# A hybrid decoder block on one NeuronCore: operands opened inside a convolution, a row root in two pieces, V's turns and the last square in another place

## The chip, the cores and the metric

The kernel runs on one core of a Trainium2 chip. A core has engines with instruction queues of their own: TensorE (PE: matmuls, and PEld, the loading of their stationary operand), VectorE (DVE), ScalarE (ACT), GpSimd (POOL) and SyncE (SP, which here only issues DMAs). They run side by side and wait for each other through semaphores. Matmuls add into PSUM banks; everything else lies in SBUF, and DMA queues move data between it and the chip's memory.

The metric is the time of the kernel on the device in microseconds (us), the median over its runs.

## The reference

One layer of a decoder block on x of 1 x 1024 x 1024 in float32, cut to what matters here:

```python
h = rms_norm(x, mix_norm_g)
z_a, q, k, v, gate_logits = split(h @ w_in)          # 1024 x 5888
u, vv = split(gelu(z_a))                             # 768 channels each
vv = rms_norm(vv)                                    # over the 768 channels
y_a = u * (causal 128x128 mixing of vv, per chunk and channel group, + b_s)
q, k = partial_rope(q, positions), partial_rope(k, positions)
y_b = dilated_mixture_attention(q, k, v)             # groups (128,1), (512,4), (2048,16)
merged = sigmoid(g_a) * (y_a @ w_branch_a) + sigmoid(g_b) * (y_b @ w_branch_b)
x = x + merged @ w_out
up = rms_norm(x) @ w_up                              # 1024 x 5632
a, val = up[:, :2816], up[:, 2816:]
a = causal_depthwise_conv(a, conv_w, conv_b)         # three taps along the sequence
x = x + (gelu(a) * val) @ w_down                     # 2816 x 1024
return rms_norm(x, final_norm_g)
```

## The kernel before, in words

**Products.** A float32 product is made of three matmul passes. Each operand is split into an upper part, which ACT makes by a copy to a reduced type (`to_parts`, L168; in the input projection `in_split`, L307), and a lower part, the difference from the upper one, which DVE or POOL makes (L169, L308). The passes are upper by upper, lower weight by upper, and upper weight by lower (`HIGH_FIRST`), so a product of four blocks of 128 rows has twelve matmuls with 512 columns, and its first four need only the upper parts. The three big projections besides do seven products instead of eight for a 2 x 2 partition of their operands, named P1 to P7. The operands of P6, P7 and P5 are sums or differences of the quarters (of the weights: `weight_sums`, L270 to L280; of the left operand: S1 to S4), and the results are put together by adds on DVE that read a PSUM bank. Three products go on in the bank of another one: P2 in that of P1, P4 in that of P7, P3 in that of P5.

**Order.** The order of PE is written out by hand over the whole kernel. Work between matmuls is placed with `after(lag, ...)`, which runs it when `lag` ticks have gone by; a tick is six matmuls of a product. On DVE and ACT the order is written out by hand at the start (up to the tenth product in `in_order`), from the merge to the end of the fourth unit of the up projection, and over the end of the up projection, the beginning of the down projection and its last product. In the later stretches lower parts on DVE stand in a list, `waiting`, and `low(n)` lets `n` of them go. Elsewhere a scheduler places DVE and ACT; POOL is left to it throughout. Queues run in the order they are given: SP issues most DMAs, ACT and POOL a few.

**Stages.** (1) `beginning()`: the first two units of the input projection run as plain products on x while its row norms are made; a unit is a pair of 128-column blocks of `w_in`. For each half of the sequence, `square_row` sums squares on ACT, `root` (L384) turns four columns of sums (one for each block of 128 rows) into the row scale on POOL, in two instructions (L387, L388), `diagonal` puts the scale on a diagonal (on DVE, L397, for the first half; on ACT, L399, for the second), `spread` (L405) broadcasts it with matmuls, and `scale_x` scales the transposed x. `in_left` then splits the quarters and sums of x, and S1 to S4. (2) `in_product` (L512, its matmuls L523, its adds L543 to L552) does the other units product by product; `in_ahead` loads and opens their weights, and `meanwhile(i)` (L1201) holds what is done on DVE and ACT beside the first sixteen products. `chain` in it is a list of small steps on DVE and ACT that make the rotary tables out of the positions; `some(n)` does the next n of them, `wide` and `turns` finish the tables. Units 0 to 2 are V of the spatial gating (kind "zv"): `turn_v` (L635) turns it with four PE transposes (L640) and ACT's Gelu out of PSUM (L645), `norm_v` and `spatial` go on from there. Rope (`turned`, L725) follows each "qa" unit. (3) Attention, the spatial gating and the gates run beside the units; then the merge and the output projection. (4) The up projection: `up_product` (L1864, matmuls L1875) with a unit of gate and value columns at a time. Its order has, for unit ff, P6(ff), P1(ff+1), P7(ff), P5(ff), P2(ff+1), P4(ff), P3(ff), without P1 and P2 of unit ff + 1 in the first units. `up_ahead` loads weights and opens operands: the sums on POOL (L275, L276, L277; on DVE in units 1 and 4), the upper part on ACT (L168), the lower part on DVE for P2, P5 and P4 and otherwise on POOL (on DVE in units 1 and 4 and for P1 of the first three). After P2 and P4 `convolve` (L1800) does the causal convolution: a first tap on ACT (L1809), two taps on DVE (L1813, L1817), and the Gelu on ACT (L1806); P4 and P3 then multiply on POOL (L1908 and L1912). `sums_g` (L1834) makes sums of finished columns for the down projection. (5) The down projection (`down_step`, L2134); with its last product, P3, each block of 128 rows ends in `down_done`: an add (L2202), `square` (L2159), `finish_block` with `finish_rms` (L2255, the root on POOL), a scaling on ACT (L2167) with ACT's DMA issue (L2168), one on DVE and SP's DMA issue.

`up_product` has a parameter `beside`, a function that `convolve` calls ahead of its Gelu. The first units use it in places (`beginning_up`), and so do P4 of the units behind the last P2; the loop from L2090 on does not use it up to the last P2.

## Time and profile before

| what | value |
| --- | --- |
| median of 3 runs | 1381.47 us (1381.35 to 1382.63) |
| profiled execution | 1382.45 us |
| its span, from the first instruction to the last | 1380.7 us |
| PE, 0 to 26 us / 26 to 140 us, busy | 24.34 of 26 / 111.47 of 114 us |
| PE, 140 to 770 us, busy | 629.3 of 630 us |
| PE, 770 to 1160 us, busy | 386.77 of 390 us |
| PE, 1160 to 1373 us, busy | 212.82 of 213 us |
| ACT, share of the span that it is busy | 47% |
| POOL, share of the span that it is busy | 22% |

The profile is that of one execution. "Busy" is time in which an engine computes; issuing a DMA, waiting and branching are not counted. A line of the profile names the line of the kernel, the engine, the operation, output and inputs by their names in the program (buffer numbers left out), and shapes. What stands in brackets behind a row is the idle time of that engine just before and the event that ended it. The granted clock is the share of full speed at which PE was let run; a matmul with 512 columns starts 0.227 us after the one before it at clock 1.00, and 0.43 us at 0.51. In a row of a timeline, an instruction's time is that from its start to its end, and instructions of one line that follow each other are shown as one piece with their count. Pieces of PE overlap a little, as matmuls are pipelined, so lengths of products are read from start to start.

### The profile page before, as it was taken

The numbers are of one execution on the slowest core, as the hardware profiler recorded it, in microseconds if no ns is written. First come the engines' busy times: TensorE is split into PE (matmuls) and PEld (weight loads), VectorE is DVE, ScalarE is ACT, GpSimd is POOL, SyncE is SP. The second block draws the span as 40 slices with busy tenths as digits, with TensorE's granted clock in tenths as the row PEclk, the third lists the DMA queues.
The fourth block names the chain that finished last, engine by engine and source line by source line (L and its number), as shares of the span: only waits on it lengthen the run. The fifth ranks groups of instructions, "written<-read, shape, count | busy, mean of one in ns | idle before, by whom it ended". The sixth has DMA issues, their size and how long they took to land.

```text
span 1380.7 us, 19226 instructions
## 1 busy us (share of the span) xinstructions
PE 1364.7 (99%) x6428; PEld 1129.2 (82%) x6428; DVE 1033.8 (75%) x1884; ACT 655.8 (47%) x1294; POOL 300.8 (22%) x295
## 2 busy tenths in 40 slices
PE   9999999999999999999999999999999999999997
PEld 7777888888888888888888886888888888888886
DVE  7978687777877887759789877666766667676674
ACT  8782455555543334444456344333333335454453
POOL 0111000000230000220011235665556643000002
PEclk9999999999999999999999999999999999999999
DMA  9435443554537995884741133233333327986663
GB/s 353 92 95 165 135 137 117 141 174 124 142 102 270 319 298 192 281 291 145 251 147 60 61 99 115 92 115 115 105 102 106 123 97 252 391 312 221 198 206 122
DMA packets 144595, 237.01 MB, mean 172 GB/s; under 512 B 13808, under 2 KB 58608, under 8 KB 144496
## 3 DMA queue, kind: packets, MB, share of 16 engines
q1 hardware_dynamic: 141968, 231.53, 50.5%
q0 software_dynamic: 1088, 2.10, 0.9%
q10 hardware_dynamic: 1440, 2.16, 0.4%
q8 instruction: 51, 0.84, 0.3%
q14 instruction: 48, 0.39, 0.1%
HBM read 167.77 MB, written 64.29 MB: 168 GB/s over the span
## 4 chain that ended last, share of the span: by engine, by line
PE 80%; DVE 8%; DMA 5%; issue 3%; ACT 2%; POOL 1%; SPq 1%; POOLq 0%; DVEq 0%; ACTq 0%
PE in_P L523 23%; PE uP L1875 17%; PE dn L2134 13%; PE up L1875 7%; PE pa L1348 5%; PE wo_P L1709 4%; PE pu L868 2%; PE pu L1855 2%; PE pb L1348 2%; DMA wd<-in_w_down_dram 1%; DMA YC<-in_x_dram 1%; PE pp L852 1%; DMA wT<-wd 1%; DMA X<-in_xt_dram 1%; DVE wd L1019 1%
## 5 line engine op out<-in xcount | busy, mean ns | idle before, releaser
L523 PE MATMUL in_P<-R,G 128*128 128x512 f32 x1008 | 246.1, 395 | 0.4 <-ACT C L543 0.3
L523 PEld LDWEIGHTS in_P<-R,G 128*128 128x128 f32 x1008 | 184.8, 188 | 37.3 <-ACT C L543 0.8
L2134 PE MATMUL dn<-R 128*128 128x512 f32 x924 | 209.6, 389 | 0.0
L2134 PEld LDWEIGHTS dn<-R 128*128 128x128 f32 x924 | 173.5, 188 | 36.0
L168 ACT ACTIVATE R<-up 128x512 fp32r<-128x512 f32 x130 | 78.5, 626 | 128.2 <-DVE up L277 42.1
L307 ACT ACTIVATE G<-wr 128x512 fp32r<-128x512 f32 x126 | 79.0, 628 | 102.2 <-PE in_P L523 63.4
L1875 PE MATMUL uP<-R 128*128 128x512 f32 x504 | 122.0, 391 | 2.7 <-POOL R L169 2.1
L523 PE MATMUL in_P<-G,G 128*128 128x512 f32 x504 | 122.2, 393 | 0.2 <-DVE C L550 0.2
L1875 PE MATMUL up<-G,R 128*128 128x512 f32 x504 | 121.5, 391 | 0.5 <-ACT R L168 0.3
L1875 PE MATMUL uP<-G,R 128*128 128x512 f32 x504 | 121.6, 390 | 0.0
L1875 PEld LDWEIGHTS uP<-R 128*128 128x128 f32 x504 | 94.7, 188 | 23.1 <-POOL R L169 2.5
L1875 PEld LDWEIGHTS up<-G,R 128*128 128x128 f32 x504 | 94.5, 188 | 21.8 <-ACT R L168 0.8
L308 DVE TENSOR_TENSOR G<-wr,G 128x512 fp32r<-128x512 f32 x126 | 88.4, 703 | 30.8 <-ACT G L307 29.8
L1875 PEld LDWEIGHTS uP<-G,R 128*128 128x128 f32 x504 | 94.5, 188 | 20.5 <-ACT R L168 0.4
L523 PEld LDWEIGHTS in_P<-G,G 128*128 128x128 f32 x504 | 92.9, 188 | 19.8 <-issue 1.2
L169 POOL TENSOR_TENSOR R<-up,R 128x512 fp32r<-128x512 f32 x55 | 84.6, 1538 | 71.8 <-ACT R L168 71.8
L169 DVE TENSOR_TENSOR R<-up,R 128x512 fp32r<-128x512 f32 x75 | 64.0, 855 | 20.7 <-ACT R L168 20.5
L168 ACT ACTIVATE R<-db 128x512 fp32r<-128x512 f32 x77 | 48.0, 625 | 56.4 <-PE dn L2134 46.8
L169 DVE TENSOR_TENSOR R<-db,R 128x512 fp32r<-128x512 f32 x77 | 53.7, 701 | 25.9 <-ACT R L168 25.7
L1348 PE MATMUL pa<-R,G 128*128 128x512 f32 x288 | 67.9, 389 | 0.0
L1348 PEld LDWEIGHTS pa<-R,G 128*128 128x128 f32 x288 | 54.1, 188 | 11.2
L523 PE MATMUL in_P<-G 128*128 128x512 f32 x252 | 62.6, 394 | 0.4 <-DVE C L552 0.2
(282 smaller groups left out, 2402.5 us busy)
## 6 DMA issues: line engine op xcount, KB each, us to landing
wr<-in_w_in_dram SPq DMA_DIRECT2D x44, 512.0 KB, 4.3
up<-in_w_up_dram SPq DMA_DIRECT2D x44, 512.0 KB, 3.6
dA<-gd SPq DMA_DIRECT2D x55, 256.0 KB, 4.8
wd<-in_w_down_dram SPq DMA_DIRECT2D x44, 256.0 KB, 5.5
wT<-wd SPq DMA_DIRECT2D x44, 256.0 KB, 3.9
dS<-gS SPq DMA_DIRECT2D x44, 256.0 KB, 4.3
db<-wT SPq DMA_DIRECT2D x44, 256.0 KB, 4.7
gd<-Y SPq DMA_DIRECT2D x42, 256.0 KB, 2.0
```

Of the source, the lines that this page charges most:

```text
L168: nc.scalar.activation(hi, src, AF.Copy)
L169: fn = lambda: lo_eng.tensor_tensor(lo, src, f32(hi), ALU.subtract)
L307: lambda: nc.scalar.activation(op[:, 0], src, AF.Copy),
L308: lambda: nc.vector.tensor_tensor(op[:, 1], src, f32(op[:, 0]), ALU.subtract),
L523: nc.tensor.matmul(acc, op[:, w, kt, :], left[LEFT[name], kt][:, a, :], start=opened and i == 0, stop=i == len(HIGH_FIRST) - 1, skip_group ...
L852: nc.tensor.transpose(pp[:, i * P : (i + 1) * P], self.pr[:, h, s * P : (s + 1) * P], ident)
L868: nc.tensor.matmul(pu[:, h * HD : (h + 1) * HD], self.pT[:, i, :], vt[:, h * HD : (h + 1) * HD], start=i % n == 0, stop=i % n == n - 1,)
L1348: nc.tensor.matmul(acc, unit[a][kt // 4][:, kt % 4, :], two(R, 8 * h + kt)[:, b, :], start=n == 0 and i == 0, stop=n == len(kts) - 1 and i ...
L1709: nc.tensor.matmul(acc, left[LEFT[name], kt][:, a, blk * P : (blk + 1) * P], out_ops[s][:, w, :], start=name not in SHARED and kt == 0 and ...
L1855: nc.tensor.matmul(acc, plain_up[which, k][:, w, kt, :], left[f"A{h + 1}{k + 1}", kt][:, a, :], start=n == 0 and i == 0, stop=n == KT - 1 ...
L1875: nc.tensor.matmul(acc, op[:, w, kt, :], left[LEFT[name], kt][:, a, :], start=opened and i == 0, stop=i == len(HIGH_FIRST) - 1, skip_group ...
L2134: nc.tensor.matmul(accs[blk], dops[s][:, 0, a, blk * P : (blk + 1) * P], dops[s][:, 1, w, :], start=SEQ[j] not in CONTINUES and kt == 0 an ...
```

## The change

The changes, by the place at which they take effect:

- `root` works on the first three columns and then on the fourth, with four POOL instructions instead of two, for each half of x.
- In `beginning`, three matmuls more (`plain_step`) go ahead of `spread(0)`; steps of the rotary chain stand at other places; the DMA that loads the positions is a step of that chain, behind the one that loads `chan`. For the first unit with seven products (unit 2) the sums for P6 stand where its split stood, ahead of P1, and P6's split behind the sum for P4. `in_op` leaves out sums that are made already (`summed`).
- In `meanwhile`, unit 2's P7 is split around S3's parts; the last lower part of S1 and of A22 stands one product later, behind that product's add; unit 3's P6 has its sums at i = 6 and its split one tick later; the ends of the rotary chain, `wide` and `turns` stand one product later.
- V's turns: those of unit 2 come 4 to 6 ticks after the result instead of 2 or 3, those of unit 0 one tick later. Rope comes 12 ticks after its loads instead of 10.
- In the up projection, P2 of unit 5 and P4 of unit 4 open an operand inside `convolve`, ahead of the Gelu.
- `finish_rms` takes the engine of its second small step: DVE in the last norm, POOL as before in the one ahead of the up projection.
- In `down_done`, the last square of a block stands ahead of the scaling and storing of the block before it.

```diff
@@ -291,7 +291,10 @@
         weight_sums(st_a, st_v, t3s, key, name, t3_tile, sum_eng)
         to_parts(op[:, 0], op[:, 1], weight_src(st_a, st_v, t3s, key, name), lo_eng)
 
+    summed = set()
+
     def in_sums(n, name):
+        summed.add((n, name))
         weight_sums(
             raws[n, 0], raws.get((n, 1)), in_t3, n, name,
             lambda: wt.tile([P, HALF], F32, name=f"wt3_{n}", tag="t3", bufs=1), nc.vector,
@@ -309,7 +312,8 @@
         )
 
     def in_op(n, name):
-        in_sums(n, name)
+        if (n, name) not in summed:
+            in_sums(n, name)
         hi, lo = in_split(n, name)
         hi()
         lo()
@@ -384,8 +388,10 @@
     def root(h):
         me = small.tile([P, 4], F32, name=f"me_x{h}", tag="me4", bufs=2)
         rs = rss[h] = small.tile([P, 4], F32, name=f"rs_x{h}", tag="rs4", bufs=2)
-        nc.gpsimd.tensor_scalar(me, mss[h], 1.0 / D, EPS, ALU.mult, ALU.add)
-        nc.gpsimd.tensor_tensor(rs, me, mhalf.to_broadcast([P, 4]), ALU.pow)
+        for cs in (slice(0, 3), slice(3, 4)):
+            n = cs.stop - cs.start
+            nc.gpsimd.tensor_scalar(me[:, cs], mss[h][:, cs], 1.0 / D, EPS, ALU.mult, ALU.add)
+            nc.gpsimd.tensor_tensor(rs[:, cs], me[:, cs], mhalf.to_broadcast([P, n]), ALU.pow)
 
     dgs = [C[1][:, i, upper] for i in range(2)]
 
@@ -608,7 +614,7 @@
         if kind == "zv":
             if (i, h) in ((0, 1), (1, 0)):
                 for bb in range(2):
-                    after(2 + bb, lambda b=4 * h + 2 * bb: turn_v(p, ct, b))
+                    after(5 + bb if h else 4 + bb, lambda b=4 * h + 2 * bb: turn_v(p, ct, b))
             if (i, h) == (1, 0):
                 for b in range(NB):
                     after(10 + 2 * b, lambda b=b: norm_v(b))
@@ -747,7 +753,7 @@
             for r, o, d0 in ((0, "q", 0), (32, "k", 0), (64, "q", 32), (96, "k", 32)):
                 nc.sync.dma_start(qkd[g, o][d0 : d0 + 32, :], t[r : r + 32])
 
-        after(10, rope)
+        after(12, rope)
 
 
     scratch = {g: dram.tile([S, UW], F32, name=f"scr{g}") for g in (1, 2)}
@@ -1109,6 +1115,8 @@
         for kt in range(KT):
             k, n = divmod(kt, QK)
             if kt % 2 == 0:
+                if kt == 2:
+                    some(1)
                 for i in range(2):
                     op, ks = plain_ops[0, k, i], slice(n, n + 2)
                     src = raws[0, i][:, kt : kt + 2]
@@ -1120,13 +1128,15 @@
                         raw[0, kt][1]()
             else:
                 raw_parts(0, kt)
-                some(2)
+                if kt > 3:
+                    some(3)
             for p in range(3):
                 for i in range(2):
                     plain_pass(0, 0, i, k, n, p)
         for kt in range(KT):
             raw_parts(1, kt)
-            some(1)
+            if kt < QK:
+                some(1)
         plain_final(0, 0, 0)
         plain_final(0, 0, 1)
         for b in range(4):
@@ -1134,7 +1144,7 @@
         load_rows(1)
         root(0)
         product(0, 1, 0)
-        some(10)
+        some(14)
         diagonal(0)
         weight(1, 0, 0)
         weight(1, 1, 0)
@@ -1142,8 +1152,9 @@
         weight(1, 1, 1)
         product(0, 1, 1, (0,))
         plain_step(0, 1, 1, 1, 0)
+        plain_step(0, 1, 1, 1, 1)
         bc0 = spread(0)
-        for kt in range(1, QK):
+        for kt in range(2, QK):
             plain_step(0, 1, 1, 1, kt)
         for kt in range(KT):
             scale_x(0, kt, bc0)
@@ -1180,9 +1191,12 @@
         parts_of("S2", range(2))
         plain_final(1, 1, 0)
         product(1, 1, 1, (0,))
-        in_ahead(0, 9, 3)
+        in_sums(FIRST, "P6")
+        in_product(FIRST, "P1")
         in_sums(FIRST, "P4")
-        in_product(FIRST, "P1")
+        for fn in in_split(FIRST, "P6"):
+            fn()
+        in_ready["op"] += 1
         product(1, 1, 1, (1,))
         for kt in range(2, QK):
             x_sum(2, kt)
@@ -1200,19 +1214,24 @@
 
     def meanwhile(i):
         if i == 0:
-            parts_of("S3")
+            split_of(FIRST, "P7")
+            late[FIRST, "P7"][0]()
+            parts_of("S3", range(2))
+            late[FIRST, "P7"][1]()
+            parts_of("S3", range(2, QK))
             in_ahead(0, 9, 5)
             late["S1"] = [in_left("S1", kt, Z[:, kt]) for kt in range(QK)]
             for hi, _ in late["S1"]:
                 hi()
         elif i == 2:
-            for _, lo in late["S1"]:
+            for _, lo in late["S1"][:3]:
                 lo()
             split_of(FIRST, "P4")
             late[FIRST, "P4"][0]()
         elif i == 3:
+            late["S1"][3][1]()
             late[FIRST, "P4"][1]()
-            for _, lo in a22:
+            for _, lo in a22[:3]:
                 lo()
             late["S4"] = [in_left("S4", kt, quarter(0, 1, kt)) for kt in range(QK)]
             for hi, _ in late["S4"]:
@@ -1220,6 +1239,7 @@
             split_of(FIRST, "P3")
             late[FIRST, "P3"][0]()
         elif i == 4:
+            a22[3][1]()
             late[FIRST, "P3"][1]()
             for _, lo in late["S4"]:
                 lo()
@@ -1233,24 +1253,36 @@
             open_zv()
             for b in range(0, NB, 2):
                 after(min(4 + b // 2, 6), lambda b=b: turn_v(1, C[1], b))
-                after(8 + b // 2, lambda b=b: turn_v(0, C[0], b))
+                after(9 + b // 2, lambda b=b: turn_v(0, C[0], b))
         elif i == 5:
             in_ahead(i, 9, 0)
             late[FIRST + 1, "P1"][1]()
         elif i == 6:
-            in_ahead(i, 9, 3)
-            some(steps_left() - 1)
+            in_ahead(i, 9, 2)
+            in_sums(FIRST + 1, "P6")
+
+            def sixth():
+                split_of(FIRST + 1, "P6")
+                for fn in late[FIRST + 1, "P6"]:
+                    fn()
+                some(7)
+
+            after(1, sixth)
         elif i == 7:
             in_ahead(i, 9, 4)
         elif i == 9:
+            some(steps_left() - 1)
+        elif i == 10:
             some(99)
-        elif i == 10:
-            for fn in wide[:8]:
+            for fn in wide[:4]:
                 fn()
         elif i == 11:
-            for fn in wide[8:]:
+            for fn in wide[4:10]:
                 fn()
-        elif i in (12, 13, 14, 15):
+        elif i == 12:
+            for fn in wide[10:]:
+                fn()
+        elif i in (13, 14, 15, 16):
             turns.pop(0)()
 
     ordered = ExitStack()
@@ -1663,7 +1695,7 @@
 
     def norm_h(b):
 
-        scales[b] = finish_rms(nc, small, mhalf, sqs2[b], f"n2_{b}")
+        scales[b] = finish_rms(nc, small, mhalf, sqs2[b], f"n2_{b}", nc.gpsimd)
 
     def scale_h(b):
         xn = xns[b] = [temp(f"xn_{b}_{c}") for c in range(2)]
@@ -2092,8 +2124,13 @@
             continue
         if i <= last_p2:
             up_ahead(i + 9, i + 4)
-            up_product(ff, name)
-            low(len(waiting))
+            if written[0] and name in ("P2", "P4"):
+                made = len(waiting)
+                up_product(ff, name, lambda: up_ahead(i + 9, i + 5))
+                low(made)
+            else:
+                up_product(ff, name)
+                low(len(waiting))
             if i == 29:
                 end_order(last_b)
         else:
@@ -2161,7 +2198,7 @@
             nc.vector.tensor_tensor(Y[:, b, cs], Y[:, b, cs], final_bc[:, cs], ALU.mult)
 
     def finish_block(b):
-        rs = finish_rms(nc, small, mhalf, sqs[b], f"f_{b}")
+        rs = finish_rms(nc, small, mhalf, sqs[b], f"f_{b}", nc.vector)
 
         def scale_and_store():
             nc.scalar.activation(Y[:, b, lower], Y[:, b, lower], AF.Copy, scale=rs)
@@ -2200,9 +2237,9 @@
             finish_block(4 + blk)()
         else:
             tt(q12, q12, acc, ALU.add)
+            square(blk, 1)
             while finished:
                 finished.pop(0)()
-            square(blk, 1)
             finished.append(finish_block(blk))
 
     banks_d, finished = {}, []
@@ -2247,12 +2284,12 @@
     pe_order.close()
 
 
-def finish_rms(nc, small, mhalf, sq, name, n=2):
+def finish_rms(nc, small, mhalf, sq, name, last):
 
     me = small.tile([P, 3], F32, name=f"fm_{name}", tag="me")
     before = EPS
-    for i in range(n):
-        nc.gpsimd.tensor_scalar(
+    for i, eng in enumerate((nc.gpsimd, last)):
+        eng.tensor_scalar(
             me[:, i : i + 1], sq[:, i : i + 1], 1.0 / D, before, ALU.mult, ALU.add
         )
         before = me[:, i : i + 1]
@@ -2285,8 +2322,8 @@
         step(nc.vector.tensor_copy, k, v)
         step(nc.vector.tensor_tensor, v, v, k, ALU.subtract)
 
-    nc.scalar.dma_start(pos, positions)
     late_load()
+    steps.append(lambda: nc.scalar.dma_start(pos, positions))
     for i, f in enumerate(INV_FREQ):
         nc.gpsimd.memset(freq[:, i : i + 1], f)
     step(nc.vector.tensor_copy, posT, pos)
```

## The prediction

> **What bounds the kernel.** I read the page first, then the waits of TensorE, then stretches by engine, and last the timeline around each wait.
>
> ```profile
> span 1380.7 us, 19226 instructions
> PE 1364.7 (99%) x6428; PEld 1129.2 (82%) x6428; DVE 1033.8 (75%) x1884; ACT 655.8 (47%) x1294; POOL 300.8 (22%) x295
> ```
> The order of the matmuls is fixed and the change takes none away (the compiled order of the changed kernel has the same ones), so only time in which TensorE (PE) stands, a slow clock, or the tail behind the last matmul can be won: 16.0 us by this row, some of it before the first matmul. The view of the waits names three places, the up projection, the start and V's transposes; the stretches (length; busy us and count of PE, PEld, DVE, ACT, POOL; granted clock, DMA) say how much is there:
>
> ```profile
> 56.00:75.00 19.00, 18.27 (x76) 13.64 (x76) 18.59 (x31) 13.77 (x25) 1.22 (x1) 1.00 0.49 108
> 92.00:140.00 48.00, 48.00 (x277) 37.66 (x276) 39.95 (x89) 20.57 (x49) 6.64 (x13) 1.00 0.49 146
> 844.00:848.00 4.00, 1.37 (x5) 0.67 (x4) 1.84 (x3) 1.72 (x4) 3.73 (x4) 1.00 0.26 101
> 849.30:852.70 3.40, 3.40 (x10) 2.61 (x9) 1.67 (x2) 0.63 (x1) 2.66 (x3) 0.51 0.20 77
> 860.00:900.00 40.00, 40.00 (x177) 32.96 (x177) 27.06 (x38) 16.56 (x27) 23.30 (x17) 1.00 0.31 105
> 1372.90:1380.70 7.80, 0.00 (x0) 0.00 (x0) 2.06 (x3) 2.17 (x4) 0.87 (x3) 0.64 0.37 143
> ```
> PE is full at clock 1.00 nearly everywhere. The sore place is 840 to 853 us: 1.37 us of work in 4.00 us, and then 3.40 us at clock 0.51. Smaller ones lie before 82 us, where DVE is full (18.59 of 19.00). The tail is 7.80 us without a matmul.
>
> **Part 1, the up projection** (`up_product` with `beside`). Single rows of the timeline there (start, us busy, engine and line; in brackets the idle time before and what ended it), of PE, then ACT, POOL and DVE:
>
> ```profile
> 837.16 3.16 PE L1875 MATMUL uP<-G,R 128*128 128x512 f32 x12
> 840.67 1.19 PE L1875 MATMUL up<-G,R 128*128 128x512 f32 x4 [0.34 <-ACT R L168]
> 844.76 1.20 PE L1875 MATMUL uP<-R 128*128 128x512 f32 x4 [0.59 <-ACT R L168]
> 848.07 2.65 PE L1875 MATMUL uP<-R 128*128 128x512 f32 x8 [2.10 <-POOL R L169]
> 850.52 3.99 PE L1875 MATMUL uP<-opx,R 128*128 128x512 f32 x12
> 854.35 2.91 PE L1875 MATMUL up<-G,R 128*128 128x512 f32 x12
> 857.09 2.88 PE L1875 MATMUL uP<-G,R 128*128 128x512 f32 x12
> 859.81 2.43 PE L1875 MATMUL uP<-R 128*128 128x512 f32 x10
> ```
> ```profile
> 835.70 0.76 ACT L1809 ACTIVATE Y<-up,chan 128x512 f32<-128x512 f32 x1
> 839.46 0.63 ACT L1806 ACTIVATE Y<-Y 128x512 f32<-128x512 f32 x1 [1.39 <-DVE Y L1813]
> 840.00 0.61 ACT L168 ACTIVATE R<-up 128x512 fp32r<-128x512 f32 x1
> 843.56 0.63 ACT L1806 ACTIVATE Y<-Y 128x512 f32<-128x512 f32 x1 [2.24 <-DVE Y L1817]
> 844.10 0.61 ACT L168 ACTIVATE R<-t 128x512 fp32r<-128x512 f32 x1
> ```
> ```profile
> 836.85 3.03 POOL L169 TENSOR_TENSOR R<-up,R 128x512 fp32r<-128x512 f32 x2
> 846.75 1.27 POOL L169 TENSOR_TENSOR R<-t,R 128x512 fp32r<-128x512 f32 x1
> 847.97 1.76 POOL L169 TENSOR_TENSOR R<-up,R 128x512 fp32r<-128x512 f32 x1
> ```
> ```profile
> 846.82 1.74 DVE L1834 TENSOR_TENSOR own<-Y 128x512 f32<-128x512 f32 x1 [2.16 <-POOL Y L1908]
> 853.47 0.68 DVE L1896 TENSOR_TENSOR Y<-Y,uP 128x512 f32<-128x512 f32 x1
> ```
> From 854.35 to 859.81 a product of twelve takes 2.73 us. P6 of unit 5, P1 of unit 6, and P7 and P5 of unit 5 should thus last 10.9 us; from 837.16 to 854.35 they last 17.2. The excess is 6.3 us: 4.7 up to 850.52, nearly all waits, and 3.83 instead of 2.73 for P5, and some of P7, in the slow clock.
>
> The cause stands in ACT's order. The upper part of unit 6's P1 (840.00) is behind the Gelu of 839.46, which waits for DVE's taps; that of unit 5's P7 (844.10) is behind the Gelu of 843.56. POOL makes the lower parts in order, so P7's (846.75) is behind the two gate products; the second, L1908, ends when L1834 starts on DVE, at 846.8. The change opens both operands ahead of those Gelus. P1's upper part then follows the first tap (835.70 + 0.76) and is done near 837.1; its lower part follows unit 5's P6 split, the first of the two from 836.85, and ends at 839.7. PE asks for them at 840.2 and, four matmuls later, at 841.1. P7's upper part follows one Gelu and one tap and is done near 840.1; POOL makes unit 5's P3 and P7 parts next, and at 1.27 to 1.76 us each the second ends between 842.3 and 843.2; PE asks for it near 843.8. Both waits go, and with them what slows the clock.
>
> What is moved back: the Gelu by two or three ACT instructions of 0.6 us, but it still ends by 838.8, before the 840.1 of now; the two gate products by two splits. Behind these wait DVE's L1834, then L276, L277 and the add of P7 (L1896), which PE's P4 of unit 5 needs, since P4 goes on in P7's bank. Now it ends at 854.15, 2.9 us before P4 (857.09). P4 would start near 851.1; stepping POOL's chain (gate products to 845.8, one split to 847.3, the sum L275 to 848.6) and DVE's (L276 and L277 at 0.7 to 1.74 each, L1896 0.68), I get the add done between 850.7 and 851.8. So 0 to 0.7 us may come back; I take 0.3. Another 0.3 stays anyway: P6's own second half starts when its split lands (838.2). Sum: 6.3 - 0.3 - 0.3 = 5.7 us, bounds 3.9 (the rival of the shared port) and 6.0.
>
> A rule that says otherwise of the clock: the Trainium skill, "TensorE: Matmul & The Clock Gate", section "What's actually happening", lets the clock halve after an idle window of about 3.4 us that runs free. The row shows 3.40 us at 0.51, as long as that window, but the longest standstill before it is 2.1 us. By the page the dip would depend on the phase, and some 1.6 us of the gain would come and go between runs.
>
> **Part 2, the start.**
>
> ```profile
> 25.63 0.20 POOL L387 TENSOR_SCALAR me_x<-ms_x 128x4 f32<-128x4 f32 x1 [24.03 <-ACT YC L380]
> 25.91 1.03 POOL L388 TENSOR_TENSOR rs_x<-me_x,mhalf 128x4 f32<-128x4 f32 x1
> 26.98 0.87 DVE L397 TENSOR_SCALAR C<-ident,rs_x 128x128 f32<-128x128 f32 x4 [2.06 <-POOL rs_x L388]
> 27.32 1.16 PE L405 MATMUL rs_bc<-C,ones 128*128 128x128 f32 x8 [1.01 <-DVE C L397]
> 88.99 0.57 POOL L199 TENSOR_TENSOR rs_v<-me_v,mhalf 128x1 f32<-128x1 f32 x1
> ```
> The last row block comes late, so the root over four columns starts at 25.63. Three columns now go ahead; the fourth costs about 0.20 and, like the 128x1 root, 0.57, so its diagonal ends near 26.75 instead of 27.85, and PE has three more matmuls (0.68 us) first and arrives near 26.8. The gain is 1.17 us (start to start), but at the second spread PE comes before ACT's diagonal (35.54 to 36.82 now, 0.45 earlier then) and 0.45 goes again: 0.7 is left. Behind it the stage hangs on DVE (18.59 of 19.00):
>
> ```profile
> 35.54 1.28 ACT L399 ACTIVATE C<-ident,rs_x 128x128 f32<-128x128 f32 x4 [0.38 <-POOL rs_x L388]
> 55.80 0.69 DVE L308 TENSOR_TENSOR G<-wr,G 128x512 fp32r<-128x512 f32 x1 [0.70 <-ACT G L307]
> 75.25 0.66 PE L640 MATMUL vt<-ident,C 128*128 128x128 f32 x4 [0.32 <-ACT C L539]
> 80.92 0.66 PE L640 MATMUL vt<-ident,C 128*128 128x128 f32 x4 [0.49 <-ACT V L645]
> ```
> DVE gains 0.45 from the diagonal and 0.70 where the sum for P4 now fills the idle time before 55.80; it loses up to 0.9 where S3's lower parts wait for ACT, which makes P7's upper part first. The last lower parts of S1 and A22 now follow an add; stepping these, P5 and P4 of the first unit each wait about 0.9 us for one, and PE reaches the first transpose of V 0.5 us earlier, no more. The turns then put matmuls between transposes: of the waits before 75.25 and 80.92 (0.32 and 0.49 idle, 1.15 start to start) about 0.3 stays. Sum of part 2: 0.5 + 0.85 = 1.35 us; bounds -0.5 (the new waits come in full, the turns give 0.3 only) and 2.7 (all named waits go). One ACT table load less, the positions' DMA behind `chan`, and the rotation steps and rope two ticks later lie beside a PE that is full (48.00 of 48.00); without that cover a rope step costs 0.7 us. The rope's four DMAs on SP move with it; the loads that read them come over ten products later: nothing.
>
> **Part 3, the tail.**
>
> ```profile
> 1372.86 0.69 DVE L2202 TENSOR_TENSOR Y<-Y,dn 128x512 f32<-128x512 f32 x1 [1.37 <-PE dn L2134]
> 1374.12 0.63 ACT L2159 ACTIVATE fj<-Y 128x512 f32<-128x512 f32 x1 [0.41 <-ACT Y L2167]
> 1374.94 0.27 POOL L2255 TENSOR_SCALAR fm_f<-fsq,fm_f 128x1 f32<-128x1 f32 x1 [1.99 <-ACT fj L2159]
> 1376.63 0.37 ACTq L2168 DMA_DIRECT2D out_dram<-Y  x1
> ```
> The last square waits for the scaling of the block before and its DMA issue; ahead of them it starts behind its own add at 1373.58, 0.54 earlier, and the small step on DVE saves 0.1 to 0.2. ACT then has that scaling and issue still to do, so the last issue comes near 1376.0: 0.6 us won (0.3 to 0.75). Elsewhere DVE's extra 128x1 steps stand before an instruction that waits for the same root anyway.
>
> **Sum.** 5.7 + 1.35 + 0.6 = 7.65 us. The profiled execution took 1382.45 us (span 1380.7), so 1374.8 us. The median of the runs, 1381.47, is 0.98 lower; I keep to the profiled one.
>
> **Rivals.**
> (a) The shared port takes 2 us of part 1 back: DVE and POOL slow each other (L1834 1.74 us against the 0.69 of L308; a split 1.76 against 1.27), and POOL's splits now stand back to back beside DVE's taps. Two DVE steps slowed by 1.1 us beyond what I stepped put the P7 add near 853 and make P4 wait 1.8 us: 1376.6 us. For it: these rows. Against: the adds from PSUM show 0.68 there. The Trainium skill, "SBUF — State Buffer", section "Who interferes with whom", states that a DVE step with two SBUF inputs and a POOL step that reads SBUF exclude each other for the whole instruction; the trace agrees (1.74 us is nearly 0.68 + 1.27).
> (b) The start gives nothing or loses 0.5, since DVE bounds it: 1376.2 to 1376.7.
> (c) Part 1 does not do what it says: P7's lower part is late all the same. Then only 0.85 of waits go and the dip stays: with the rest, about 1379.7. Against: POOL's compiled order has that split ahead of both gate products.
> (d) Slower: the pause at 844 let POOL and DVE get ahead; without it, the wait of P4 for P7's add returns in every later unit. It decides from 0.62 us a unit on, over 17 units 10.5 us: 1385. For it: nothing but the thin first margin. Against: from 860 to 900 POOL is busy 23.30 and DVE 27.06 of 40.00, so both catch up within a unit.
>
> **Numbers.** Forecast 0.62, (a) 0.14, (b) 0.11, (c) 0.06, (d) 0.07. A change of 0.2% (2.8 us) is about what a measurement of this kernel can tell from none. (c) is half within it: faster 0.89, within 0.03, slower 0.08, with some left for what I do not see. The range goes from 1372.3 (upper bounds of all parts, 9.45, and a little of the 0.98) to 1378.0 ((a) and (b) together).
>
> **What would show it.** Right: no wait of PE on POOL's L169 near 844, no stretch of clock 0.5 there, the twelve-matmul starts 2.73 us apart from unit 5's P6 on; rs_bc without 1.0 us before it; the last square right behind its add. Wrong: PE waiting for DVE's P7 add, a clock dip elsewhere, waits over 1 us between 60 and 71 us.

## The result and the profile after

The changed kernel took 1378.8 us (median of 7 runs, 1376.24 to 1380.19), the kernel before 1382.79 us in the runs beside it (7 runs, 1381.35 to 1383.94). The ratio is 0.997, with an interval of 0.9959 to 0.9982: 4.1 us less, between 2.5 and 5.7. I had forecast 7.65 us less and 1374.8 us, and the range ended at 1378.0.

The profiled execution was the fastest of the seven, 1376.24 us. Its page begins so:

```profile
span 1374.5 us, 19220 instructions
PE 1361.9 (99%) x6428; PEld 1128.5 (82%) x6428; DVE 1036.5 (75%) x1892; ACT 654.3 (48%) x1293; POOL 297.5 (22%) x291
```
The view of the waits of PE (who waited for whom: total us, times, longest) has lost POOL's L169 and has got two others:

```profile
PE uP L1907 <- DVE Y L1928: 1.9, 1, 1.9
PE in_P L529 <- DVE G L432: 1.2, 2, 0.7
```
L1907 is the matmul of the up projection, L1928 the add of P7, L432 the lower part of a left operand. The stretches, with the columns as in the prediction:

```profile
56.00:75.00 19.00, 17.77 (x77) 13.55 (x76) 18.07 (x30) 13.50 (x24) 1.21 (x1) 1.00 0.48 109
92.00:140.00 48.00, 48.00 (x277) 37.66 (x276) 39.19 (x87) 19.72 (x50) 5.97 (x12) 1.00 0.47 146
842.30:846.30 4.00, 4.00 (x20) 3.26 (x18) 1.22 (x2) 1.49 (x3) 3.44 (x3) 1.00 0.54 215
848.00:852.00 4.00, 2.09 (x10) 1.41 (x9) 3.10 (x3) 1.66 (x3) 2.63 (x3) 1.00 0.17 66
860.00:900.00 40.00, 40.00 (x178) 32.96 (x177) 26.87 (x40) 16.16 (x26) 24.96 (x19) 1.00 0.32 104
1367.50:1374.50 7.00, 0.00 (x0) 0.00 (x0) 2.32 (x4) 2.06 (x4) 0.55 (x1) 0.84 0.51 198
```
The stretch that had 1.37 us of matmuls in 4.00 (now 1.5 us earlier, at 842.3) is full and the clock stays at 1.00. A new hole stands at 848 to 852: 2.09 us of matmuls in 4.00. The tail is 7.0 us instead of 7.8. Between 56 and 75 us PE is no fuller than before (17.77 against 18.27).

The rows around the new hole, from the timeline of PE, DVE and POOL:

```profile
838.55 2.88 PE L1907 MATMUL up<-G,R 128*128 128x512 f32 x12
841.27 2.88 PE L1907 MATMUL uP<-R 128*128 128x512 f32 x12
843.99 2.93 PE L1907 MATMUL uP<-opx,R 128*128 128x512 f32 x12
846.75 2.93 PE L1907 MATMUL up<-G,R 128*128 128x512 f32 x12
851.59 3.02 PE L1907 MATMUL uP<-G,R 128*128 128x512 f32 x12 [1.91 <-DVE Y L1928]
```
```profile
838.29 1.79 DVE L1845 SCALAR_TENSOR_TENSOR Y<-Y,chan 128x511 f32<-128x511 f32 x1
840.01 1.26 DVE L1849 SCALAR_TENSOR_TENSOR Y<-edge,chan,Y 128x1 f32<-128x1 f32 x1
845.43 1.78 DVE L1866 TENSOR_TENSOR own<-Y 128x512 f32<-128x512 f32 x1 [2.78 <-POOL Y L1940]
848.40 0.69 DVE L276 TENSOR_TENSOR up<-up,up 128x512 f32<-128x512 f32 x1 [0.59 <-POOL t L275]
849.12 1.81 DVE L277 TENSOR_TENSOR up<-up 128x512 f32<-128x512 f32 x1
850.86 0.68 DVE L1928 TENSOR_TENSOR Y<-Y,uP 128x512 f32<-128x512 f32 x1
```
```profile
839.49 1.75 POOL L169 TENSOR_TENSOR R<-t,R 128x512 fp32r<-128x512 f32 x1
842.86 1.29 POOL L1936 TENSOR_TENSOR Y<-Y 128x512 f32<-128x512 f32 x1 [1.61 <-ACT Y L1838]
844.11 1.29 POOL L1940 TENSOR_TENSOR Y<-Y 128x512 f32<-128x512 f32 x1
846.62 1.74 POOL L275 TENSOR_TENSOR t<-up 128x512 f32<-128x512 f32 x1
849.11 1.28 POOL L169 TENSOR_TENSOR R<-t,R 128x512 fp32r<-128x512 f32 x1 [0.74 <-ACT R L168]
```
P1 and P7 start without a wait, 2.72 us apart, as forecast. P4 of unit 5 would start at 849.5 (2.73 us behind P2's 846.75) and starts at 851.59, because P7's add (L1928) ends at 851.54. It stands in DVE's queue behind the sums L276 and L277 of unit 6; these wait for POOL's L275, that one stands behind the two gate products and a split, and the gate products wait for a Gelu that waits for DVE's taps. A tap of a single column (128x1) takes 1.26 us there; it ends at 841.27, just after POOL's split (841.24). In before the same two taps and the same sum were these, the first tap and the sum each with a split of POOL beside them in part:

```profile
841.36 1.19 DVE L1813 SCALAR_TENSOR_TENSOR Y<-Y,chan 128x511 f32<-128x511 f32 x1 [1.39 <-ACT Y L1809]
842.47 0.21 DVE L1817 SCALAR_TENSOR_TENSOR Y<-edge,chan,Y 128x1 f32<-128x1 f32 x1
851.73 1.82 DVE L277 TENSOR_TENSOR up<-up 128x512 f32<-128x512 f32 x1
```

### The profile page after: what moved, and what is told of

It reads as the page before. It is cut to its first block, busy times and chain, and to the rows that moved or that the text cites. A ratio compares the mean times of both kernels' runs of the same rounds, so it can differ in the third digit from the quotient of the medians.

```text
span 1374.5 us, 19220 instructions
## 1 busy us (share of the span) xinstructions
PE 1361.9 (99%) x6428; PEld 1128.5 (82%) x6428; DVE 1036.5 (75%) x1892; ACT 654.3 (48%) x1293; POOL 297.5 (22%) x291
## 4 chain that ended last, share of the span: by engine, by line
PE 91%; DVE 3%; DMA 2%; ACT 1%; POOL 1%; issue 1%; SPq 0%; ACTq 0%; DVEq 0%; POOLq 0%
PE in_P L529 28%; PE uP L1907 20%; PE dn L2171 15%; PE up L1907 8%; PE pa L1380 5%; PE wo_P L1741 5%; PE pu L874 2%; PE pu L1887 2%; PE pb L1380 2%; PE pp L858 1%; DMA YC<-in_x_dram 1%; PE sc L819 1%; PE sc L820 1%; DMA X<-in_xt_dram 1%; PE pm L683 1%
## 5 line engine op out<-in xcount | busy, mean ns | idle before, releaser
L1907 PE MATMUL uP<-G,R 128*128 128x512 f32 x504 | 121.7, 390 | 1.9 <-DVE Y L1928 1.9
L1907 PE MATMUL up<-G,R 128*128 128x512 f32 x504 | 121.1, 391 | 0.0
L1907 PE MATMUL uP<-R 128*128 128x512 f32 x504 | 121.1, 389 | 0.0
L1907 PEld LDWEIGHTS uP<-G,R 128*128 128x128 f32 x504 | 94.4, 188 | 22.7 <-DVE Y L1928 2.3
L1907 PEld LDWEIGHTS up<-G,R 128*128 128x128 f32 x504 | 94.6, 188 | 20.6
L1907 PEld LDWEIGHTS uP<-R 128*128 128x128 f32 x504 | 94.6, 188 | 19.6
L169 POOL TENSOR_TENSOR R<-up,R 128x512 fp32r<-128x512 f32 x55 | 83.9, 1526 | 66.2 <-ACT R L168 66.2
L169 DVE TENSOR_TENSOR R<-up,R 128x512 fp32r<-128x512 f32 x75 | 64.2, 858 | 18.6 <-ACT R L168 18.4
L169 DVE TENSOR_TENSOR R<-db,R 128x512 fp32r<-128x512 f32 x77 | 53.6, 699 | 26.2 <-ACT R L168 25.9
```

The source lines that it names most:

```text
L169: fn = lambda: lo_eng.tensor_tensor(lo, src, f32(hi), ALU.subtract)
L1907: nc.tensor.matmul(acc, op[:, w, kt, :], left[LEFT[name], kt][:, a, :], start=opened and i == 0, stop=i == len(HIGH_FIRST) - 1, skip_group ...
```

## The experiments

Runs of one kernel lie up to 4 us apart, so single terms are read from the traces: the start of the same matmul, counted from the first, in the kernel's trace minus that in the trace of before (us; negative is earlier); the marks are times in before. "Tail" is the change of the time from the start of the last matmul to the end of the span. Between 900 us and the last matmul no kernel differs from before by more than 0.01 us.

| kernel | up to 74 us | 74 to 140 | 140 to 830 | 830 to 900 | tail |
| --- | --- | --- | --- | --- | --- |
| after | 0.01 | -0.94 | -0.64 | -3.79 | -0.81 |
| again | 1.51 | -0.90 | 1.12 | -3.76 | -0.81 |
| again_2 | 0.04 | -0.94 | 1.66 | -3.73 | -0.82 |
| up_only | -0.61 | 0.01 | 2.02 | -3.69 | -0.01 |
| start_only | 0.52 | -0.90 | -1.35 | 0.00 | -0.01 |
| tail_only | -0.33 | 0.01 | 1.33 | -0.01 | -0.80 |
| p4_only | 0.56 | 0.01 | 0.93 | -2.94 | -0.02 |
| order_36 | -0.18 | -0.89 | 2.27 | -1.45 | -0.81 |
| order_36b | -0.79 | -0.89 | -0.38 | -5.32 | -0.82 |
| unit5_dve | 0.86 | -0.89 | -0.63 | -5.05 | -0.81 |
| unit5_order | 0.44 | -0.89 | -0.04 | -5.47 | -0.82 |
| root_only | -1.29 | 0.00 | -0.12 | -0.13 | -0.01 |
| lows_back | 0.13 | -0.90 | -0.07 | -3.73 | -0.81 |
| chain_apart | 0.05 | -0.91 | 1.11 | -3.69 | -0.82 |
| pos_first | -0.18 | -0.90 | 0.11 | -3.74 | -0.81 |
| chain_old | -1.09 | -0.93 | -0.44 | -2.15 | -0.80 |
| combo | -0.13 | -0.90 | -0.64 | -5.09 | -0.81 |
| order_chain | -0.86 | -0.90 | -1.41 | -5.32 | -0.80 |

### The three parts, each alone, and the changed kernel again

`up_only` has the hunk at `up_product` alone, `start_only` all hunks ahead of 140 us, `tail_only` those of `finish_rms`, `norm_h`, `finish_block` and `down_done`; `again` and `again_2` are the changed kernel.

> The kernel before with the operands of the up projection opened inside the convolution, and nothing else. Prediction: 5.7 us less. By the trace of the changed kernel (waits and slow clock of 6.3 us go, 2.07 us come back as P4's wait for P7's add): 3.8 us less. If that wait sets off a slow stretch of the clock in most runs: about 2 us less.

> The kernel before with the changes ahead of 140 us alone (root, splits, sums, V's turns, rope and the rotary chain). Prediction: 1.35 us less, between 0.5 more and 2.7 less. By the trace of the changed kernel, whose matmuls stand 0.93 us earlier from 140 us on: 0.9 us less; 1.8 less if the 0.9 us lost before 25 us is scatter of the loads, and 0 if it belongs to the change and the rest is scatter.

> The kernel before with the last square ahead of the other block's scaling, and the second small step of the last norm on DVE. Prediction: 0.6 us less (0.3 to 0.75). By the trace of the changed kernel: the tail behind the last matmul goes from 7.8 to about 7.0 us, so 0.8 less. If the issue of the other block's store only moves behind the root: no change.

> The changed kernel once more, for a second trace. Its seven runs lay between 1376.24 and 1380.19 us, and the one with the trace was the fastest. Theory A (the trace is typical, the runs only scatter): the new trace looks like the first, with the 2.07 us wait of P4 for P7's add near 850 us, clock 1.00 all along, and a span of 1374 to 1376 us. Theory B (a slow stretch of the clock comes and goes): a trace with a span of 1376.5 to 1378.5 us shows some 3.4 us at a clock near 0.5, worth 1.7 us, somewhere behind a wait of PE; the likeliest place is behind the wait for P7's add. Theory C (the loads at the start scatter): the excess stands before 30 us instead.

> The changed kernel a third time, for the slow stretch of the clock: of six traces with the single wait of 2.06 us before P4, five showed clock 1.00 behind it and one 3.4 us at 0.51. If that depends on where the wait falls in a period of the clock's own, this trace shows either, and with it 1.6 us more in that place; if it depended on the kernel's start, this one shows none, as the changed kernel did twice.

Measured against before: `up_only` 0.9984 (0.9974 to 0.9994), `start_only` 0.9998 (0.999 to 1.0007), `tail_only` 0.9992 (0.9983 to 1.0), `again` 0.9973 (0.9962 to 0.9983). In four traces with it, part 1 shortens 830 to 900 us by 3.7 to 3.8 us, and the wait of P4 is 2.05 to 2.08 us in each: not chance, and part of the change. The tail gives 0.8. The start gives nothing that the times can tell. The times of `up_only` are 2.2 us less (0.8 to 3.6), a little under what its trace shows for 830 to 900 us; the three parts by their times make 3.6 us, against 4.1 for the changed kernel.

The three traces of the changed kernel span 1374.5, 1377.9 and 1376.9 us. None shows a slow clock behind 100 us; the second lost 1.5 us ahead of 74 us, and the second and third lost 1.1 and 1.7 us between 140 and 830 us, where the change moves little or nothing that PE waits for. So `again`'s theory C (the loads at the start) holds for part of the excess, B nowhere, and the stage behind 140 us was in none of its theories; `again_2` ran once, 1378.63 us, without a slow stretch. What happens between 140 and 830 us, the view of `up_only` (DVE and PE) shows:

```profile
476.79 0.69 DVE L1019 TENSOR_TENSOR wd<-wd,wd 128x512 f32<-128x512 f32 x1 [3.03 <-DMA wd<-in_w_down_dram]
```
```profile
480.03 3.00 PE L523 MATMUL in_P<-G,G 128*128 128x512 f32 x12 [2.50 <-DVE C L550]
```
DVE waits for a load of `w_down`, and the add that PE needs (L550) is queued behind that. Over 19 traces this stage scatters from 1.4 us shorter to 2.3 us longer than in the trace of before. That the load's landing causes the scatter is read from such rows and not shown; I didn't try to move it.

### What takes part 1's gain back

`order_36` writes the order of DVE and ACT out through unit 5, so that P7's add goes ahead of unit 6's sums; `order_36b` also opens the operands of unit 6 and 7 inside the convolution:

```diff
-            if written[0] and name in ("P2", "P4"):
+            if i < 30 and name in ("P2", "P4"):     # order_36; order_36b keeps the line above
...
-            if i == 29:
+            if i == 36:
                 end_order(last_b)
```


> The changed kernel with the order of DVE and ACT written out by hand through unit 5 of the up projection, so that P7's add of unit 5 stands ahead of the two sums for unit 6 (and ahead of the sum for the down projection). Theory A (P4 waits because that add is queued behind sums that wait for POOL): the add is done by 846 us, P4's wait of 2.07 us is gone, and from unit 5's P6 to unit 6's P6 the matmuls gain 2.0 us on the changed kernel. Theory B (DVE as a whole is late there, whatever the order): a wait of 1 to 2 us stays, before P4 or before the next unit's P6, whose operand is now opened later. Time about 2 us under the changed kernel by A, the same by B.

> As the kernel with the order written out through unit 5, and the operands of P1 of unit 7 and P7 of unit 6 opened inside the convolution too. Theory A (the stall of 2.9 us and the slow clock that came back in unit 6 have the cause of the stall of before: P7's upper part behind a Gelu, its lower part behind both gate products): the stall leaves unit 6, and 900 us is reached 4 to 5 us ahead of that kernel if it does not come back in unit 7. Theory B (the engines behind PE fall behind by some 2 us in any order, and the wait only moves): a stall of 2 us or more stands in unit 6 or 7.

Rows of `order_36`: DVE's add of P7; then PE, at P2 of unit 6 and P4 of unit 5, and one unit later at P7 of unit 6; then the stretch behind that:

```profile
847.23 0.68 DVE L1928 TENSOR_TENSOR Y<-Y,uP 128x512 f32<-128x512 f32 x1
```
```profile
849.31 2.93 PE L1907 MATMUL up<-G,R 128*128 128x512 f32 x12
852.08 2.88 PE L1907 MATMUL uP<-G,R 128*128 128x512 f32 x12
863.60 1.20 PE L1907 MATMUL uP<-R 128*128 128x512 f32 x4 [0.48 <-ACT R L168]
866.90 2.98 PE L1907 MATMUL uP<-R 128*128 128x512 f32 x8 [2.10 <-POOL R L169]
```
```profile
868.00:871.40 3.40, 3.40 (x10) 2.67 (x9) 1.54 (x2) 0.63 (x1) 2.66 (x3) 0.52 0.22 82
```
The add ends at 847.9 and P4 (852.08) starts 2.77 us after the product ahead of it: its wait is gone, and from 830 to 860 us 6.2 us are won, nearly all of the 6.3 us of excess that the prediction counted. But 4.8 of them go again in unit 6, in the form that unit 5 had before: P7 waits for ACT, then 2.10 us for POOL's lower part, and then the clock is slow for 3.4 us. Both theories were half right: the order of the queue decided P4's wait, and the old stall moves on to the first unit whose P7 operand is opened behind the Gelu. With that operand opened too (`order_36b`) 0.7 us is left of it, again a wait of P4 for L1928, and 5.3 us stay won: 1375.0 us, ratio 0.9939 (0.9926 to 0.9953). `order_36` took 1378.87 us (0.9975, 0.9965 to 0.9985).

`unit5_dve` lets DVE make unit 5's sums and lower parts, and `unit5_order` joins that to `order_36b`:

```diff
-        free = nc.vector if ff in (1, 4) else nc.gpsimd
+        free = nc.vector if ff in (1, 4, 5) else nc.gpsimd
```


> The changed kernel with all of unit 5's sums and lower parts on DVE, so that POOL makes no splits beside DVE's taps; DVE gets about six more steps of 0.7 us. Theory A (DVE and POOL exclude each other, and this made the taps and sums late): the taps of unit 4 take 0.75 us instead of 1.79, the 128x1 step 0.15 us instead of 1.26, P7's add of unit 5 ends 1 to 3 us earlier, and P4's wait shrinks to under 1 us. Theory B (the queue is late for its own work): with more work on DVE the add is later still and P4 waits 3 us or more.

> The changed kernel with unit 5's sums and lower parts on DVE, the order of DVE and ACT written out through unit 5, and P1 of unit 7 and P7 of unit 6 opened inside the convolution. If the late P7 add and the late operands are all there is, no stall of over 0.5 us stands between 835 and 900 us and that stretch is 5.5 to 6.2 us shorter than before. If DVE with its additional steps is the bound, waits of 1 to 2 us for its lower parts (P5, P4 of unit 5, P6 of unit 6) take their place.

DVE in `unit5_dve`, the same taps, sum and add:

```profile
839.74 0.74 DVE L1845 SCALAR_TENSOR_TENSOR Y<-Y,chan 128x511 f32<-128x511 f32 x1
840.40 0.21 DVE L1849 SCALAR_TENSOR_TENSOR Y<-edge,chan,Y 128x1 f32<-128x1 f32 x1
848.73 1.84 DVE L277 TENSOR_TENSOR up<-up 128x512 f32<-128x512 f32 x1
850.50 0.67 DVE L1928 TENSOR_TENSOR Y<-Y,uP 128x512 f32<-128x512 f32 x1
```
With POOL idle beside them the taps take 0.74 and 0.21 us instead of 1.79 and 1.26; the sum L277, still beside a split of POOL, takes 1.84. With six more steps of its own DVE ends P7's add 1.3 us sooner (counted from P6's start), and P4 waits 0.2 us instead of 2.07; the rest of that difference is PE's own delay, since P6 now waits 0.6. This is what the Trainium skill says in "SBUF — State Buffer", sections "SBUF: two separate sides" and "Who interferes with whom": a DVE step with two SBUF inputs and a POOL step that reads SBUF exclude each other for the whole instruction. The trace agrees down to the tap of one column, which lasted until the split was over. `unit5_dve` took 1376.2 us, 0.996 (0.9946 to 0.9975). `unit5_order` has no wait over 0.3 us there and wins 5.5 us: 1375.12 us, 0.994 (0.9927 to 0.9954).

`p4_only` is `up_only` with only P7's operand ahead of its Gelu:

```diff
+            if written[0] and name == "P4":        # up_only: name in ("P2", "P4")
```

> The kernel before with P7's operand of unit 5 opened inside the convolution of unit 4's P4, while P1's of unit 6 stays behind the Gelu. Theory A (two separate waits): the stall of 3.0 us before and in P7 goes, with the slow clock, and the 0.85 us wait of P1 stays; P4's wait for P7's add comes, by about 1.2 us as PE is 0.85 later. Theory B (the one opened first pushes the other): P7's lower part is late still, by 1 us or more.

Its waits of PE include

```profile
PE uP L1875 <- DVE Y L1896: 1.7, 1, 1.7
```
P7's stall and the slow clock are gone, P1's waits of 0.50 and 0.35 us (start to start) are there as before, and P4 waits 1.82 us instead of the 1.2 expected: theory A, with P4's wait a little larger. P7's operand is worth 2.9 of the 3.75 us. The kernel ran once, 1380.96 us.

### The start

`root_only` is the kernel before with the hunk of `root` and the added matmuls:

```diff
+        for cs in (slice(0, 3), slice(3, 4)):
...
         plain_step(0, 1, 1, 1, 0)
+        plain_step(0, 1, 1, 1, 1)
         bc0 = spread(0)
-        for kt in range(1, QK):
+        for kt in range(2, QK):
```

> The kernel before with the row root in two pieces and one more block of matmuls ahead of the spread, and nothing else of the start. Prediction: 1.17 us won at the first spread, 0.45 lost again at the second, 0.7 left at 56 us. By the traces so far, where kernels with the whole changed start win 1.0 to 1.3 between 25 and 30 us and lose 0 to 1.5 by 56 us: 0.4 to 1.0 left. If the second spread is bound by ACT's squares and the loads before them: 0 left at 56 us.

Its PE, 24 to 40 us:

```profile
25.25 1.52 PE L586 MATMUL pl<-R,G 128*128 128x512 f32 x6
26.61 1.05 PE L407 MATMUL rs_bc<-C,ones 128*128 128x128 f32 x8
27.41 7.76 PE L586 MATMUL pl<-R,G 128*128 128x512 f32 x33
35.01 1.08 PE L407 MATMUL rs_bc<-C,ones 128*128 128x128 f32 x8
```
Neither spread waits. From 25 to 56 us it wins 1.25 us and up to 140 us it keeps 1.07: more than forecast, and the second spread takes nothing back. That is one execution (1380.9 us), and its last square on ACT ended at 33.34 us, the earliest of all 19 traces (34.12 in before). In the nine traces with the whole changed start the second spread takes back 0 to 1.46 us, 0.47 in the mean, and 25 to 55 us end up 0.66 us shorter in the mean (from 1.28 shorter to 0.48 longer).

`lows_back` puts the last lower parts of S1 and A22 back ahead of the adds:

```diff
-            for _, lo in late["S1"][:3]:
+            for _, lo in late["S1"]:
...
-            late["S1"][3][1]()
...
-            for _, lo in a22[:3]:
+            for _, lo in a22:
...
-            a22[3][1]()
```

> The changed kernel with the last lower parts of S1 and A22 back ahead of the adds. By the trace of the changed kernel, P5 and P4 of the first unit with seven products wait 0.95 and 0.70 us for these parts, and the stretch from 62 to 74 us is 0.75 us longer than before: it should be 0.5 to 0.8 us shorter here if the moved parts cost it, and as long if DVE bounds it anyway, since then the adds come later and PE waits for their banks.

The two waits of 0.95 and 0.70 us break up into five of 0.34 to 0.46, and 62 to 74 us is as long as in the changed kernel (0.76 us over before in both). So moving those parts costs nothing: with either order DVE bounds this stretch. `lows_back` took 1378.17 us, 0.9973 (0.9962 to 0.9983).

That leaves the first 25 us, where kernels with the changed start arrive 0.6 to 1.1 us late. Three kernels undo parts of the rotary chain's move: `chain_apart` the steps in a row, `pos_first` the place of the positions' DMA, `chain_old` both, with all other steps of the chain ahead of V.

```diff
 # chain_apart
-                    some(3)
+                    some(2)
...
-            if kt < QK:
+            if kt < QK + 2:
                 some(1)
 # pos_first
-                if kt == 2:
-                    some(1)
...
+    nc.scalar.dma_start(pos, positions)
     late_load()
-    steps.append(lambda: nc.scalar.dma_start(pos, positions))
```


> The changed kernel with two steps of the rotary chain instead of three beside the sixth and eighth block of the first product (and two more behind). Theory A (the 0.8 us lost before 25 us comes from ACT waiting for a step of DVE that has just been queued): ACT's idle 1.23 us before its step of the chain goes, and the matmuls stand 0.7 to 0.9 us earlier at 25 us than in the changed kernel. Theory B (it is the loads of the first weights and of x, which land later): no change at 25 us.

> The changed kernel with the rotary chain's steps ahead of V, and the positions' DMA, back where they were before (the root in two pieces, sums, splits, turns, up projection and tail stay). The kernels with the changed start reach 25 us 0.68 to 1.11 us late, the others 0 to 0.25. Theory A (the chain's places and the DMA behind `chan` cost this): 25 us is reached within 0.3 of before, the second spread then loses less than the 0.27 to 1.46 us it loses now, and 140 us is reached 1.5 to 2 us ahead of before, against 0.9 for the changed kernel. Theory B (the loads land when they will): 0.7 to 1.1 late at 25 us here as well.

> The changed kernel with only the positions' DMA back at the head of ACT's queue, ahead of `chan`; the chain's other steps stay at their new places, three beside the sixth and eighth block. In the traces with the DMA behind `chan` its queue is busy until 9.6 to 10.3 us, and the loads on SP's queue reach 4 MB (counted by its packets) at 14.8 to 16.0 us; with the DMA first, until 3.6 to 3.9 us and 14.3 to 15.3 us. Theory A (the DMA's place holds up the loads of x): its queue is done by 4 us, 4 MB come at 14.3 to 15.3 us, and the 0.6 us lost between 12 and 22.7 us go to 0.2 or less. Theory B (the three steps in a row hold ACT up): ACT still waits some 1.2 us for the chain's step on DVE, and 0.4 us or more are lost.

Lost between the matmuls that start at 11.8 and 22.7 us in before: 0.65 us in the changed kernel (0.42 to 0.81 in nine traces with both moves), 0.56 in `chain_apart`, 0.63 in `pos_first`, 0 in `chain_old` (and within 0.05 of 0 in the six others with neither move). Either move alone costs the whole, and together they cost no more; for each move alone there is one trace. The rows of ACT in the changed kernel, in `pos_first`, in `chain_apart`, and in before:

```profile
13.28 0.26 ACT L2339 ACTIVATE ones<-ones 128x64 fp32r<-128x64 f32 x1 [1.23 <-DVE ones L2318]
```
```profile
12.68 0.26 ACT L2337 ACTIVATE ones<-ones 128x64 fp32r<-128x64 f32 x1 [1.23 <-DVE ones L2316]
```
```profile
15.57 2.72 ACT L468 ACTIVATE G<-X,chan 128x512 fp32r<-128x512 f32 x4 [1.08 <-DMA X<-in_xt_dram]
```
```profile
14.56 2.74 ACT L462 ACTIVATE G<-X,chan 128x512 fp32r<-128x512 f32 x4 [0.82 <-DMA X<-in_xt_dram]
```
With three steps in a row ACT stands 1.23 us in its queue's order for a DVE step just issued, with the splits of x behind it. With the steps apart that wait is gone, but ACT waits for x itself until 15.57, against 14.56 in before. The packets fit that: with the DMA behind `chan` SP's queue has moved 4 MB after 14.8 to 16.0 us (ten traces, mean 15.5), with it first after 14.3 to 15.3 (nine, mean 14.8). So the loads come later with the moved DMA; that this alone delays the matmuls rests on the trace of `chain_apart`. My theory for `chain_apart` was wrong by itself and right as one of two. `chain_old` starts 2.0 us ahead at 140 us, as its theory A had it, and took 1376.83 us (0.9953, 0.9939 to 0.9966), though its second spread still gave back 0.33 us; `chain_apart` 1378.16 us (0.9974, 0.9962 to 0.9987), `pos_first` 1376.96 us (0.9966, 0.9954 to 0.9977).

### A version that beats both

`combo` is `chain_old` with `unit5_dve`, `order_chain` is `chain_old` with `order_36b`.

> The changed kernel with unit 5's sums and lower parts on DVE and the rotary chain's first steps back where they were. If both work as their own runs say: up projection 5.0 us under before (830 to 900 us), start 1 to 2 us, tail 0.8, so 1375 us and 6 to 7 us under before. If the chain's places give nothing: 1376.2 as with unit 5 alone.

> The changed kernel with the order written out through unit 5, the operands of P1 of unit 7 and P7 of unit 6 opened inside the convolution, and the rotary chain's first steps where they were. If the two gains add: 830 to 900 us 5.3 us shorter than before, the start 1 to 2, the tail 0.8: 1373.5 us (1372.5 to 1375). If the start's gain is lost behind DVE: 1375.0, as without it.

`combo` took 1374.65 us (5 runs, 1374.49 to 1374.84), ratio to before 0.9936 (0.9922 to 0.9949); `order_chain` 1374.27 us (6 runs, 1373.12 to 1375.59), 0.9943 (0.9929 to 0.9958). By the ratios that is 8 to 9 us under before and some 4 us under the changed kernel; between the two the intervals don't decide. `combo` lay 0.35 us under its forecast of 1375, `order_chain` within its 1372.5 to 1375, as if the gains add. The page of `order_chain` and its largest wait of PE behind 100 us:

```profile
span 1371.4 us, 19225 instructions
```
```profile
PE uP L1903 <- DVE Y L1924: 0.6, 1, 0.6
```

## Why the prediction was wrong

The direction was right and the mechanisms mostly too; two terms of the sum were mis-sized. By the traces the three parts are worth 3.75, 0.5 and 0.8 us, together 5.1 (inside the interval of the times, 2.5 to 5.7), where I had 5.7, 1.35 and 0.6.

**Part 1.** The waits for P1's and P7's operands went, and the slow clock with them; P6's own wait stayed at 0.2 us (forecast 0.3). The step that failed: "So 0 to 0.7 us may come back; I take 0.3." It measured 2.07. On the time axis of before, I had P7's add done between 850.7 and 851.8; it ended at 853.1 (851.54, and the matmuls stood 1.54 us earlier). My stepping let the gate products follow POOL's splits at once and end at 845.8. They ended at 846.9, no earlier than in before: POOL stood 1.61 us behind its last split until their Gelu came, since the splits, now beside DVE's taps, stretched two of the taps to 3.05 us together (0.95 undisturbed, 1.40 in before). Behind them L275 took 1.74 us instead of the 1.3 that I had stepped, and L277 1.81 us, just over the 0.7 to 1.74 that I had given it, though it took 1.82 in the profile of before. This is rival (a), which had the add "near 853", the wait at 1.8 us and 1376.6 us; the traced execution took 1376.24. That these totals lie so close is luck: (a) counts the start at its full 1.35 us, this execution was the fastest of seven, and the median is 2.2 us over (a). Its rows (1.74 us beside POOL against 0.69) were in the profile, and I gave it 0.14 because the adds out of PSUM keep 0.68 us there. But not the add was slow: what stood ahead of it was. Rival (d), that the wait returns in each later unit, did not come: 860 to 900 us is full.

**Part 2.** By the traces 0.5 us instead of 1.35 (at 140 us the matmuls stand 0.6 us ahead of before in the mean of nine traces with the changed start, and 0.1 in four with the old one; single traces lie between 1.7 ahead and 0.6 behind, so 0.5 is good to some 0.3). The root gave 1.1 to 1.25 in its own trace; in the changed start it gave 0.66 net of the second spread, close to my 0.7. The turns gave 0.90 (forecast 0.85). What I had costed at nothing failed: the rotary steps and the positions' DMA "lie beside a PE that is full". That row was of 92 to 140 us; these steps stand before 25 us, where ACT and the loads of x feed PE block by block. They cost 0.6 us there, and ACT's squares and with them the second spread come later (the last square ends at 35.0 us in the mean of the nine, at 34.0 in that of the three kernels with the steps taken back). With them taken back the matmuls stand 1.6 us ahead at 140 us (the mean of three traces). The two waits for lower parts came as forecast, 0.95 and 0.70 us against 0.9 each, but as another form of DVE's bound, not as a price of moving those parts. So rival (b), which let DVE bound the start and give 0 or less, came nearer in size than my forecast, and had the cause only in part.

**Part 3.** 0.8 us, a little over the bound of 0.75. The last square stands right behind its add (a wait of 1.38 us for the add, none for the scaling), and ACT's last DMA issue comes 3.26 us behind the end of the last matmul instead of 3.80, 0.54 us won where I had 0.6:

```profile
1368.22 0.63 ACT L2196 ACTIVATE fj<-Y 128x512 f32<-128x512 f32 x1 [1.38 <-DVE Y L2239]
1370.72 0.35 ACTq L2205 DMA_DIRECT2D out_dram<-Y  x1
```
From that issue to the end of the span it is 3.80 us instead of 4.07 (in all traces with the changed tail and in all without it, within 0.01), which I had not counted; why is open. The square's place and the step on DVE were not run apart.

**The range.** (a) and (b) came together, the case at which my range ended, 1378.0, and the median lay 0.8 us above. I had left nothing for the scatter of this kernel: the three runs that I saw lay within 1.3 us, the seven of the changed kernel within 4.0.

**The clock.** I had written that the slow stretch might come and go. The double stall of before (0.65 to 0.77 and 2.27 us over, within 4.5 us) was followed by one in all five traces that have it. Nine traces have a single wait of P4 of 1.8 to 2.1 us, and one of them, `chain_old`, has the slow stretch behind it, with 1.6 us lost:

```profile
851.30:854.70 3.40, 3.40 (x10) 2.62 (x9) 3.15 (x6) 1.79 (x3) 1.85 (x2) 0.51 0.00 0
```

## What to carry to other kernels

A stall that is removed was also slack for the engines behind it: step the queue of whoever frees the next bank with the durations that its instructions take beside the neighbour's work, not with their best ones, and let the add that frees a bank go ahead of sums that wait for another engine. Cost a moved step by the row of the place to which it goes; a cover that holds at 100 us says nothing of the first 25, where a DMA or a chain of small steps on two engines delays the splits that feed TensorE. Where runs scatter as much as the terms of the sum, compare the start of the same matmul at a few marks in each trace: in the three traces of the changed kernel the terms of 74 to 140 us, of 830 to 900 us and of the tail agree within 0.1 us though the totals differ by 3.

## What was not expected of the hardware

The slow clock lasted 3.4 us at 0.51 to 0.52 each time, as after the standstill in the prediction. The Trainium skill, "TensorE: Matmul & The Clock Gate", section "What's actually happening", asks for an idle window of about 3.4 us that runs free; here a wait of 2.06 us was enough in one trace of nine, and two waits in a row (in before with 1.37 us of matmuls in 4.00) were enough in five of five. The length agrees with that window, the standstill needed does not. In the quietest 3.41 us (the length of the slow stretch) of each trace there, matmuls filled 1.19 to 1.20 us in the five with two waits, 1.47 to 1.53 us in eight of the nine with one (`chain_old` 1.51) and 1.76 us in the ninth, `p4_only`; so this count parts the five from the others, but not `chain_old`, and what decides in the single case stays open.
